# Layer 0's modulation vectors: from TensorE products to VectorE sums inside the window attention

## The chip, the cores and the metric

One core of one Trainium2 chip runs the whole program: a two-layer block of a diffusion transformer, in float32. The metric is device time in microseconds (us) of one execution; the time before is 2756.34 us, the median of three runs. The engines are called by the profile's names: PE (TensorE, matrix products), PEld (its weight loads), DVE (VectorE), ACT (ScalarE), POOL (GpSimd) and SP (SyncE, which here issues every transfer, in order, on one queue).

## The reference, cut to what matters

Both layers scale and shift their normalised activations with a modulation computed from a conditioning vector. There are two streams, the latent tokens (1024) with the vector `c` and the context tokens (256) with `c_ctx`:

```python
mod_l = (jax.nn.silu(c) @ ada_w[layer] + ada_b[layer]).reshape(batch, 1, N_MOD, D_MODEL)
mod_c = (jax.nn.silu(c_ctx) @ ada_w[layer] + ada_b[layer]).reshape(1, 1, N_MOD, D_MODEL)
h_l = modulate(x, norm1_g[layer], mod_l, 0)          # chunks 0 and 1
y_c, y_l = ab_mixer(h_c, h_l, ...)                   # mLSTM and banded window attention
x = x + mod_l[:, :, 2] * y_l                         # chunk 2
x = x + mod_l[:, :, 5] * sq_relu_mlp(modulate(x, norm2_g[layer], mod_l, 3), ...)   # chunks 3, 4, 5
```

`ada_w[layer]` is 1024 x 6144: six chunks of 1024 columns, 24 MB in float32. Chunks 0 and 1 of layer 0 are needed at the very start. The subject here is chunks 2 to 5 of layer 0 (16 MB): chunk 2 at the residual after the mixer, 3 and 4 at the second norm, 5 only when the MLP's second matrix is added to the residual. Layer 1's six chunks are needed after layer 0's MLP.

The window attention of layer 0 has 8 heads of 64 (two per pass, four passes), 10 query blocks of 128 tokens, each block against the context (256 keys) and up to three neighbouring key blocks.

## The kernel before, in words

Tokens lie on the free axis, channels on the 128 partitions. The large products use a split of each float32 operand into a rounded part and a remainder and three products (`mm3`, L436; lines L442 to L444), each 128x128 weights against 512 or 256 columns. SBUF holds one big tile `F` (8592 columns, written in pages of `PG` = 1024 and half pages `H` = 512), tiles `W` for split weights, and `x`, `hhi`, `hlo` for activations. PSUM is one tile of 8 banks; `Banks` hands out banks by letter, and `Area` hands out places of `F` by tag in rotation, so a tile waits for the last reader of the place that it takes.

The stages on the path: `front` (an order written out by hand, with the modulation chunks 0 and 1, keys, values and the first queries), then `swa` (L1808), the window attention with what fills it, then the mLSTM with the output projection, then `mlp` for layer 0 (`mlp_hidden`, then `mlp_out`), then layer 1. Outside the blocks under a manual schedule, the framework's scheduler orders each engine's instructions by its own estimates of their durations; a constraint can be given with `issue_after(ins)`, which puts an instruction behind another one on the same engine and makes no semaphore wait.

In `swa` every one of the 40 (pass, block) turns does this: `scores` (L1816): PE makes up to 8 products into one set of three PSUM banks (L1827 to L1831), DVE takes them out with the band mask and the running maximum (L1835, L1840), ACT makes exponentials (L1850), DVE normalises (L1856). One turn later `values` transposes the result on PE (L1870), ACT and DVE split it (L416, L417 into `ptl`), PE multiplies with the values (L1876, L1877), and DVE adds the two halves (L1881). The score banks are one set, so the next block's products wait until DVE has read the last ones.

Between these turns stand fillers: `queries` (the next pass's projection), `gather` (L1791, the four mLSTM heads' projections, stored to DRAM through a small `ev` tile) and `ada_steps` (L187), which computes the modulation. `rest` (L1891) interleaves `gather` and `ada_steps`; a counter (`total`) spreads all of it evenly over the 40 turns. `ada_steps` takes a 1024-column chunk in four steps. A step loads two 128x1024 pieces of `ada_w` (512 KB each, tag `adaraw`, two places in `F`), makes four products with the two streams' conditioning vectors as 32-column weights (L200), two rows of 128 inputs by two halves of 512 columns side by side in the array, and DVE adds the result up from PSUM (L207; the first step by ACT). At the chunk's end four small products turn the row sums into columns (L212) and DVE adds the bias (L218).

Layer 1's modulation is computed otherwise, by `ada_sums` (L221), in layer 0's `mlp_hidden`: a step loads 128x512 pieces (256 KB, tag `raw`), and DVE multiplies each with one entry of the conditioning vector per partition and adds it to a running sum in PSUM (L233, L235, one instruction per stream and piece, the last one into SBUF, L240); then PE sums over the partitions with a matrix of ones (L249) and DVE adds the bias (L252). Its generator is asked for a step at three places in each pair of hidden blocks (`fill` in `pair`), from the third pair on; DVE also adds up the MLP's own products there (L665, L640).

Of the kernel before, what the change touches and what calls it, by code (L numbers as in the profile page):

```python
# [10 lines left out]
F32 = mybir.dt.float32  # L11
# [8 lines left out]
P = 128  # L20
# [95 lines left out]
class Kernel:  # L116
# [70 lines left out]
    def ada_steps(self, layer, block, wp, tp, psp, tag):  # L187


        nc, a = self.nc, self.a  # L190
        acc = tp.tile([P, 512], F32, tag="adaacc")
        for kk in range(ND // 2):
            ps = psp.tile(tag, "adaps")
            for e in range(2):
                k = 2 * kk + e
                w = wp.tile([P, 1024], F32, tag="adaraw")
                nc.sync.dma_start(w, a["ada_w"][layer, k * P : (k + 1) * P, block * 1024 : (block + 1) * 1024])
                for u in range(2):
                    q = 2 * e + u
                    nc.tensor.matmul(  # L200
                        ps[32 * q : 32 * q + 32, :], self.cs[:, k, :], w[:, u * 512 : u * 512 + 512],
                        start=True, stop=True, tile_position=(0, 32 * q),
                    )
            if kk == 0:
                nc.scalar.activation(acc, ps, AF.Copy)
            else:
                nc.vector.tensor_tensor(acc, ps, acc, op=ALU.add)  # L207
            if kk < ND // 2 - 1:
                yield
        pt = psp.tile(tag, "adapt")  # L210
        for i in range(4):
            nc.tensor.matmul(pt[:, 4 * i : 4 * i + 4], acc[:, i * P : (i + 1) * P], self.asel, start=True, stop=True)  # L212
        c0 = block * 8
        bias = self.v(V_AB + layer * 48 + c0, 8).rearrange("p (u i) -> p i u", i=4)
        src = pt[:, :16].rearrange("p (i u v) -> p i u v", i=4, u=2)
        dst = self.mod[layer][:, c0 : c0 + 8, :].rearrange("p (u i) v -> p i u v", i=4)
        for vv in range(2):
            nc.vector.tensor_tensor(dst[:, :, :, vv], src[:, :, :, vv], bias, op=ALU.add)  # L218
        yield

    def ada_sums(self, layer, block, streams, tp, psp, tag):  # L221


        nc, a = self.nc, self.a
        sums = [psp.tile(t, "adacc") for t in "XY"[:streams]]
        acc = [[tp.tile([P, n], F32, tag=f"acc{v}") for _ in range(512 // n)] for v, n in enumerate((512, 256)[:streams])]
        for k in range(ND):
            w = tp.tile([P, 512], F32, tag="raw")
            nc.sync.dma_start(w, a["ada_w"][layer, k * P : (k + 1) * P, block * 512 : block * 512 + 512])
            for v in range(streams):  # L230
                c = self.cs[:, k, v : v + 1]
                if k == 0:
                    nc.vector.tensor_scalar(sums[v], w, c, None, op0=ALU.mult)  # L233
                elif k < ND - 1:
                    nc.vector.scalar_tensor_tensor(sums[v], w, c, sums[v], op0=ALU.mult, op1=ALU.add)  # L235
                else:
                    n = 512 // len(acc[v])
                    for i, t in enumerate(acc[v]):
                        x = slice(i * n, i * n + n)
                        nc.vector.scalar_tensor_tensor(t, w[:, x], c, sums[v][:, x], op0=ALU.mult, op1=ALU.add)  # L240
            if k % 4 == 3:
                yield
# [1565 lines left out]
    def swa(self, sp, small, tb, psp, wp, mixd, heads, st, qs, band, gates):  # L1808
# [953 lines left out]
```

## Time and profile before

| what | value |
|---|---|
| three runs | 2754.09, 2756.34, 2759.79 us; median 2756.34 |
| profiled execution, its time and its span | 2762.11 us and 2760.3 us |
| mean granted TensorE clock | 0.994 |
| window attention, 150 to 530 us | PE busy 371.4, DVE 229.7, ACT 200.7, POOL 67.1 us of 380 |
| layer 0's hidden MLP, 860 to 1200 us | PE busy 336.2, DVE 211.7, POOL 206.1 us of 340 |
| products of `ada_steps` (L200) | 128 instructions, 164 to 520 us |
| sums of `ada_sums` (L233 to L249) | about 820 to 1170 us |

A float32 product appears as two matrix instructions. Busy time is the union of an engine's instructions. A busy PE isn't a PE at its peak: its instructions are pipelined, so what one costs is read from the distance of starts and not from its length. In the rows of groups the number after the bar is busy time, then the mean of one in ns, then the idle time of the engine just before them and what ended it. In a timeline, `[2.13 <-DVE small L1835]` is idle time before the row and its releaser.

### The profile page before, as it was taken

To read this page: it belongs to the slowest core of one execution; us is meant where nothing else is said; L and a number is where in the kernel's file an instruction comes from. 1 tells how busy PE (TensorE), PEld (TensorE's weight loads), DVE (VectorE), ACT (ScalarE), POOL (GpSimd) and SP (SyncE) were. 2 spreads that over 40 slices of the span, in tenths; PEclk is the share of its full clock that TensorE was granted. 3 is DMA by queue.
4 is the path that set the end of the run, shared out by engine and by line. 5 is a ranking of instruction groups with operands and counts; after the bars stand their busy time and mean duration, and the time that the engine had idled before them with its cause. 6 is when DMAs were issued, how large, how long until landed. Compare 5 with 4: busy or idle time off the path is not lost.

```text
span 2760.3 us, 40910 instructions
## 1 busy us (share of the span) xinstructions
PE 2692.7 (98%) x14757; PEld 2274.0 (82%) x14757; DVE 1882.4 (68%) x3268; ACT 1472.8 (53%) x2604; POOL 1078.8 (39%) x734
## 2 busy tenths in 40 slices
PE   8999999999999999999999999999999999999999
PEld 4787878787888888878888889999988888878877
DVE  5455556578776666558669557888874676666675
ACT  5665454444674444344437557888865554444342
POOL 2422020001246667510002347787774598720000
PEclk9999999999999999999999999999999999999999
DMA  7222223443325676497747610000155255477674
GB/s 246 87 79 91 101 87 124 160 155 109 111 91 193 198 246 217 154 333 272 257 141 259 217 47 20 24 26 20 32 182 167 69 180 194 172 281 264 215 232 148
DMA packets 194756, 427.96 MB, mean 155 GB/s; under 512 B 21176, under 2 KB 47576, under 8 KB 194552
## 3 DMA queue, kind: packets, MB, share of 16 engines
q1 hardware_dynamic: 194552, 425.34, 46.1%
q8 instruction: 116, 1.90, 0.3%
q14 instruction: 88, 0.72, 0.1%
HBM read 322.51 MB, written 102.74 MB: 154 GB/s over the span
## 4 chain that ended last, share of the span: by engine, by line
PE 74%; DVE 6%; DMA 5%; issue 2%; ACT 2%; POOL 1%; SPq 0%; DVEq 0%; POOLq 0%; ACTq 0%
PE psum L610 23%; PE psum L1089 16%; PE psum L442 4%; PE psum L443 4%; PE psum L444 4%; PE psum L2392 4%; PE psum L2582 3%; PE psum L1187 3%; PE psum L2299 3%; DMA hhiraw<-in_w 3%; DVE W L417 1%; PE psum L1870 1%; POOL W L417 1%; PE psum L2457 1%; DVE x L1094 1%
## 5 line engine op out<-in xcount | busy, mean ns | idle before, releaser
L417 POOL TENSOR_TENSOR W<-F,W 128x512 fp32r<-128x512 f32 (+2 forms) x310 | 469.3, 1528 | 514.6 <-ACT W L416 385.9
L1089 PE MATMUL psum<-W,W 128*128 128x512 f32 x2688 | 615.8, 390 | 10.6 <-DVE W L417 4.8
L1089 PEld LDWEIGHTS psum<-W,W 128*128 128x128 f32 x2688 | 502.7, 188 | 123.3 <-DVE W L417 10.7
L610 PE MATMUL psum<-hhi,W 128*128 128x512 f32 (+1 forms) x1600 | 441.9, 356 | 2.5 <-DVE x L665 1.6
L416 ACT ACTIVATE W<-F 128x512 fp32r<-128x512 f32 (+2 forms) x375 | 269.9, 735 | 285.0 <-POOL F L583 98.3
L610 PEld LDWEIGHTS psum<-hhi,W 128*128 128x128 f32 x1600 | 285.0, 189 | 46.3 <-DVE x L665 2.0
L610 PE MATMUL psum<-hlo,W 128*128 128x512 f32 (+1 forms) x800 | 284.3, 355 | 0.0
L416 ACT ACTIVATE W<-hhiraw 128x1024 fp32r<-128x1024 f32 x98 | 103.9, 1061 | 313.1 <-PE psum L1089 189.7
L442 PE MATMUL psum<-hhi,W 128*128 128x512 f32 (+1 forms) x600 | 224.4, 374 | 0.0
L444 PE MATMUL psum<-hhi,W 128*128 128x512 f32 (+1 forms) x600 | 218.3, 364 | 0.0
L443 PE MATMUL psum<-hlo,W 128*128 128x512 f32 (+1 forms) x600 | 218.0, 363 | 0.0
L417 DVE TENSOR_TENSOR W<-hhiraw,W 128x1024 fp32r<-128x1024 f32 x98 | 119.6, 1221 | 73.8 <-ACT W L416 73.2
L583 POOL TENSOR_TENSOR F<-F 128x512 f32<-128x512 f32 x112 | 164.9, 1472 | 12.4 <-DMA F<-in_w 5.4
L610 PEld LDWEIGHTS psum<-hlo,W 128*128 128x128 f32 x800 | 151.2, 189 | 21.4 <-issue 0.2
L1008 DVE TENSOR_TENSOR hhiraw<-hhiraw 128x512 f32<-128x512 f32 x154 | 104.2, 688 | 91.0 <-DMA hhiraw<-in_w 90.1
L409 POOL TENSOR_TENSOR hlo<-F,hhi 128x256 fp32r<-128x256 f32 (+1 forms) x12 | 13.1, 1088 | 301.8 <-ACT F L400 301.8
L442 PEld LDWEIGHTS psum<-hhi,W 128*128 128x128 f32 x600 | 113.7, 190 | 20.3 <-ACT x L416 2.5
L443 PEld LDWEIGHTS psum<-hlo,W 128*128 128x128 f32 x600 | 113.8, 190 | 16.7 <-issue 2.2
L444 PEld LDWEIGHTS psum<-hhi,W 128*128 128x128 f32 x600 | 113.6, 189 | 16.2 <-issue 0.2
L417 DVE TENSOR_TENSOR W<-hloraw,W 128x1024 fp32r<-128x1024 f32 x98 | 122.8, 1253 | 4.0 <-DMA hhiraw<-in_w 4.0
L610 PE MATMUL psum<-x,W 128*128 128x512 f32 x504 | 125.1, 393 | 0.0
L610 PEld LDWEIGHTS psum<-x,W 128*128 128x128 f32 x504 | 95.6, 190 | 20.4
(496 smaller groups left out, 6268.2 us busy)
## 6 DMA issues: line engine op xcount, KB each, us to landing
F<-in_w SPq DMA_DIRECT2D x104, 512.0 KB
hloraw<-hd SPq DMA_DIRECT2D x90, 512.0 KB
hhiraw<-in_w SPq DMA_DIRECT2D x72, 512.0 KB
hd<-F SPq DMA_DIRECT2D x142, 256.0 KB
hhiraw<-in_w SPq DMA_DIRECT2D x116, 256.0 KB
F<-in_ada_w SPq DMA_DIRECT2D x96, 256.0 KB
hd<-x SPq DMA_DIRECT2D x90, 256.0 KB
F<-in_win SPq DMA_DIRECT2D x32, 512.0 KB
```

The source lines that it names most:

```text
L416: nc.scalar.activation(hi, src, AF.Copy)
L417: eng.tensor_tensor(lo, src, hi.bitcast(F32), op=ALU.subtract)
L442: nc.tensor.matmul(ps, sh, mh, start=i == 0, stop=False)
L443: nc.tensor.matmul(ps, sh, ml, start=False, stop=False)
L444: nc.tensor.matmul(ps, sl, mh, start=False, stop=i == n - 1)
L583: add = lambda o, p, q, how: nc.gpsimd.tensor_tensor(o, p, q, op=how)
L610: nc.tensor.matmul(ps, w[i][:, p], B[j][k], start=first and j == 0 and m == 0, stop=last and j == 3 and m == 2)
L1008: tt = lambda o, p, q, how: eng.tensor_tensor(o, p, q, op=how)
L1089: nc.tensor.matmul(bank(base + i), A[u][:, p], B[v], start=first and m == 0, stop=last and m == 2)
L1187: nc.tensor.matmul(bank(k), B[u][:, i * P : i * P + P], A[v][:, half], start=f == 0 and m == 0, stop=f == NFF - 1 and m == 2,)
L2299: nc.tensor.matmul(ps, s[:, c], m[:, j, t0 : t0 + QT], start=j == 0 and i == 0, stop=j == ND - 1 and i == 2)
L2392: nc.tensor.matmul(u.o[:, :QT], v[x], p[y], start=c == 0 and m == 0, stop=c == 2 * NB - 1 and m == 2)
```

## The change

`ada_steps` is deleted. Layer 0's chunks 2 to 5 are now eight half chunks of 512 columns computed by `ada_sums` with both streams: six (512-column blocks 4 to 9) as fillers in the window attention, two (blocks 10 and 11, which are chunk 5) ahead of layer 1's twelve in the hidden MLP. In the attention the running sums lie in SBUF (`F`), not in PSUM; three places of 256 KB take the loads; each DVE sum is put behind the newest score block's normalisation on DVE (`pace`), and the first half chunk's loads behind the front's last store on SP (`behind`). A block in the attention has four steps of two pieces (`marks` 1, 3, 5, 7), asked for after three of five `gather` steps instead of two of five; `total` grows from 66 to 75. In the MLP a block with two streams has three steps of 3, 3 and 2 pieces where it had two of 4 and one for the turn; the turn now rides with the next block's first step.

```diff
-    def ada_steps(self, layer, block, wp, tp, psp, tag):
...
-                w = wp.tile([P, 1024], F32, tag="adaraw")
-                nc.sync.dma_start(w, a["ada_w"][layer, k * P : (k + 1) * P, block * 1024 : (block + 1) * 1024])
-                for u in range(2):
-                    q = 2 * e + u
-                    nc.tensor.matmul(
-                        ps[32 * q : 32 * q + 32, :], self.cs[:, k, :], w[:, u * 512 : u * 512 + 512],
-                        start=True, stop=True, tile_position=(0, 32 * q),
-                    )
...
-    def ada_sums(self, layer, block, streams, tp, psp, tag):
+    def ada_sums(self, layer, block, streams, tp, psp, tag, sums=None, marks=(3, 7), behind=None, pace=nullcontext):
...
+        if sums:
+            acc = [[t] for t in sums]
+        else:
+            sums = [psp.tile(t, "adacc") for t in "XY"[:streams]]
...
         for k in range(ND):
             w = tp.tile([P, 512], F32, tag="raw")
-            nc.sync.dma_start(w, a["ada_w"][layer, k * P : (k + 1) * P, block * 512 : block * 512 + 512])
+            with self.tc.issue_after(behind.ins) if behind else nullcontext():
+                nc.sync.dma_start(w, a["ada_w"][layer, k * P : (k + 1) * P, block * 512 : block * 512 + 512])
+            with pace():
+                for v in range(streams):
+                    c = self.cs[:, k, v : v + 1]
+                    if k == 0:
+                        nc.vector.tensor_scalar(sums[v], w, c, None, op0=ALU.mult)
+                    elif k < ND - 1:
+                        nc.vector.scalar_tensor_tensor(sums[v], w, c, sums[v], op0=ALU.mult, op1=ALU.add)
...
-            if k % 4 == 3:
+            if k in marks:
                 yield
...
+    def ada_pieces(self, pieces, *args, behind=None, **kw):
+
+        for layer, block, streams, marks in pieces:
+            yield from self.ada_sums(layer, block, streams, *args, marks=marks, behind=behind, **kw)
+            behind = None
         yield
...
-            nc.sync.dma_start(ud[0][1][:, s], e)
+            self.fronted = nc.sync.dma_start(ud[0][1][:, s], e)
...
-                nc.vector.tensor_scalar(sc[:, h, :nk], sc[:, h, :nk], nm[:, 5, h : h + 1], None, op0=ALU.mult)
+                paced[0] = nc.vector.tensor_scalar(sc[:, h, :nk], sc[:, h, :nk], nm[:, 5, h : h + 1], None, op0=ALU.mult)
...
-            ada = (s for b in range(2, 6) for s in self.ada_steps(0, b, wp, tb, psp, "A"))
+            F = self.F
+            sums = [tb.tile([P, 512], F32, tag="adaacc"), F[:, 4 * PG + H : 5 * PG]]
+            ad = Area()
+            ad.place("raw", cuts(F, H, 3 * PG, 3 * PG + H, 4 * PG))
+            ada = self.ada_pieces(
+                [(0, b, 2, (1, 3, 5, 7)) for b in range(4, 10)], ad, psp, "A",
+                sums=sums, behind=self.fronted, pace=lambda: self.tc.issue_after(paced[0].ins),
+            )
...
-                if i % 5 in (1, 3):
+                if i % 5 in (0, 2, 3):
...
-        total, done, left = 3 * 3 + 48 - 7 + 16, 0, 0
+        total, done, left = 3 * 3 + 48 - 7 + 25, 0, 0
...
-            steps.append(s for b in range(12) for s in k.ada_sums(1, b, 2 if b < 4 else 1, tp, psp, tag))
+            pieces = [(0, b, 2, (2, 5, 7)) for b in (10, 11)]
+            pieces += [(1, b, 2, (2, 5, 7)) if b < 4 else (1, b, 1, (3, 7)) for b in range(12)]
+            steps.append(k.ada_pieces(pieces, tp, psp, tag))
```

Three places show what this moves. The first is PE in the window attention. Before, a step's four products stand between a block's transposes (`psum<-ident,x`) and the next block's score products (`psum<-KH`, `psum<-KL`):

```order
L1830 MATMUL psum<-KH_579,x_1985 128x384
L1831 MATMUL psum<-KL_581,x_1985 128x384
L1870 MATMUL psum<-ident,x_1096 128x128 x8
L200 MATMUL psum<-F,cs 32x512 x4
L1827 MATMUL psum<-KH_579,x_1984 128x256
L1828 MATMUL psum<-KL_581,x_1984 128x256
L1830 MATMUL psum<-KH_579,x_1984 128x256
```

With the change no such row is left. Six times there are eight short products with the matrix of ones, one half chunk's turn (`psum<-hhi,W` and `psum<-hlo,W` are projections, L1803 to L1807 the score products under their new line numbers):

```order
L419 MATMUL psum<-hhi,W_106 128x256
L420 MATMUL psum<-hlo,W_106 128x256
L421 MATMUL psum<-hhi,W_106 128x256
L220 MATMUL psum<-ones,F 128x2 x8
L1803 MATMUL psum<-KH_579,x_1996 128x256
L1804 MATMUL psum<-KL_581,x_1996 128x256
L1806 MATMUL psum<-KH_579,x_1996 128x384
```

So sixteen groups of four wide products, and four groups of four turns, became six groups of eight turns on PE here.

The second is DVE in the same stage. Before, between the split of the transposed scores (`ptl`), a block's normalisation (L1856) and the next block's scores (L1835), one addition of `ada_steps` (L207):

```order
L1846 TENSOR_TENSOR small<-vec,small 128x2
L207 TENSOR_TENSOR F<-psum,F 128x512
L1853 TENSOR_TENSOR small<-small 128x2
L1854 RECIPROCAL small<-small 128x2
L1881 TENSOR_TENSOR x_1097<-psum,small 64x128
L1856 TENSOR_SCALAR x_1095<-x_1095,small 128x640 x2
L1881 TENSOR_TENSOR x_1097<-psum,small 64x128
L1835 ISA x_1096,small<-psum,kzero,vec 128x256
```

Now (L1832 is the normalisation, L1811 the next block's scores):

```order
L1829 TENSOR_TENSOR small<-small 128x2
L1830 RECIPROCAL small<-small 128x2
L394 TENSOR_TENSOR ptl<-psum,x_1098 128x256
L1832 TENSOR_SCALAR x_1096<-x_1096,small 128x640 x2
L206 SCALAR_TENSOR_TENSOR F<-F,cs 128x512
L1857 TENSOR_TENSOR x_1097<-psum,small 64x128 x2
L206 SCALAR_TENSOR_TENSOR F<-F,cs 128x512 x3
L1811 ISA x_1095,small<-psum,kzero,vec 128x256
```

Four sums stand between a normalisation and the next block's scores; there are 24 such groups in the 40 turns.

The third is SP's queue at the end of the front. Before, two loads of 512 KB stood among the front's weights:

```order
L1599 DMA F<-in_rope 128x1024
L197 DMA F<-in_ada_w 128x1024
L1516 DMA F<-in_win 128x1024
L197 DMA F<-in_ada_w 128x1024
L1516 DMA F<-in_win 128x1024
```

Now the first three, of 256 KB, stand behind the front's last stores and ahead of the band mask (`in_band`):

```order
L1726 DMA u_137<-F 128x512 x2
L1345 DMA F<-in_tri 128x2x128
L199 DMA F<-in_ada_w 128x512 x3
L1348 DMA F<-in_band 128x384
L1781 DMA u_137<-F 128x256
```

The 48 loads of the attention then go two at a time between the stores of `gather` and the weights.

More of the change, by code (lines that the diff above doesn't have):

```diff
@@ L185, in v @@
         return self.vec[:, i : i + n]
-    def ada_steps(self, layer, block, wp, tp, psp, tag):
+    def ada_sums(self, layer, block, streams, tp, psp, tag, sums=None, marks=(3, 7), behind=None, pace=nullcontext):
         nc, a = self.nc, self.a
[L191 to L195, printed above, removed]
-                w = wp.tile([P, 1024], F32, tag="adaraw")
-                nc.sync.dma_start(w, a["ada_w"][layer, k * P : (k + 1) * P, block * 1024 : (block + 1) * 1024])
-                for u in range(2):
-                    q = 2 * e + u
-                    nc.tensor.matmul(
-                        ps[32 * q : 32 * q + 32, :], self.cs[:, k, :], w[:, u * 512 : u * 512 + 512],
-                        start=True, stop=True, tile_position=(0, 32 * q),
-                    )
[L204 to L219, printed above, removed]
@@ L221, in ada_sums @@
-    def ada_sums(self, layer, block, streams, tp, psp, tag):
-        nc, a = self.nc, self.a
-        sums = [psp.tile(t, "adacc") for t in "XY"[:streams]]
-        acc = [[tp.tile([P, n], F32, tag=f"acc{v}") for _ in range(512 // n)] for v, n in enumerate((512, 256)[:streams])]
+        if sums:
+            acc = [[t] for t in sums]
+        else:
+            sums = [psp.tile(t, "adacc") for t in "XY"[:streams]]
+            acc = [[tp.tile([P, n], F32, tag=f"acc{v}") for _ in range(512 // n)] for v, n in enumerate((512, 256)[:streams])]
@@ L227, in ada_sums @@
         for k in range(ND):
             w = tp.tile([P, 512], F32, tag="raw")
-            nc.sync.dma_start(w, a["ada_w"][layer, k * P : (k + 1) * P, block * 512 : block * 512 + 512])
[L230 to L240, printed above, removed]
@@ L241, in ada_sums @@
-            if k % 4 == 3:
+            with self.tc.issue_after(behind.ins) if behind else nullcontext():
[7 more added lines that the diff above has]
+                        nc.vector.scalar_tensor_tensor(sums[v], w, c, sums[v], op0=ALU.mult, op1=ALU.add)
+                    else:
+                        n = 512 // len(acc[v])
+                        for i, t in enumerate(acc[v]):
+                            x = slice(i * n, i * n + n)
+                            nc.vector.scalar_tensor_tensor(t, w[:, x], c, sums[v][:, x], op0=ALU.mult, op1=ALU.add)
@@ L1373, in mixer0 @@
                 wp.place("raw", cuts(self.F, PG, 2 * PG))
-                wp.place("adaraw", cuts(self.F, PG, 3 * PG, 4 * PG))
                 tb.place("ev", cuts(self.F, H, 5 * PG))
```

1 line of the change is left out of this document (added).

## The prediction

> **What bounds the kernel now.** I read the page's busy shares first, then the chain that ended last, then the busy times by stage.
>
> ```profile
> span 2760.3 us, 40910 instructions
> PE 2692.7 (98%) x14757; PEld 2274.0 (82%) x14757; DVE 1882.4 (68%) x3268; ACT 1472.8 (53%) x2604; POOL 1078.8 (39%) x734
> PE 74%; DVE 6%; DMA 5%; issue 2%; ACT 2%; POOL 1%; SPq 0%; DVEq 0%; POOLq 0%; ACTq 0%
> ```
>
> PE is busy in 98% of the span and makes 74% of the chain. That is an average, so the stages that the change touches are read by themselves (columns: PE, PEld, DVE, ACT, POOL busy, granted clock, DMA share, GB/s):
>
> ```profile
> 0.00:150.00 150.00, 137.50 (x727) 92.92 (x728) 77.66 (x167) 88.06 (x162) 52.61 (x40) 0.98 0.47 158
> 150.00:530.00 380.00, 371.35 (x2235) 307.50 (x2234) 229.72 (x770) 200.74 (x455) 67.08 (x43) 0.99 0.30 100
> 860.00:1200.00 340.00, 336.18 (x1823) 291.44 (x1822) 211.74 (x302) 146.43 (x269) 206.07 (x149) 1.00 0.61 204
> ```
>
> In the window attention (150 to 530 us) PE leaves 8.6 us idle of 380, and DVE 150.3. PE is the bound there, with DVE in a loop with it. What DVE waits for is in its groups:
>
> ```profile
> L1835 DVE CUSTOM_DVE_ANT_0 x<-psum,kzero,vec 128x256 f32<-128x256 f32 x76 | 34.2, 481 | 68.2 <-PE psum L1828 68.2
> L207 DVE TENSOR_TENSOR F<-psum,F 128x512 f32<-128x512 f32 x12 | 8.2, 687 | 11.8 <-PE psum L200 11.8
> L1853 DVE TENSOR_TENSOR small<-small 128x2 f32<-128x2 f32 x38 | 7.1, 186 | 32.3 <-ACT x L1850 28.7 <-ACT small L1847 3.6
> ```
>
> Of its 150.3 us, 68.2 are waits for PE's score products and 11.8 for the modulation's products; the other 70.3 are waits inside the softmax (32.3 on the exponentials) and small ones. So DVE has some 80 us to give in this stage and no more; the rest is its own latency.
>
> **What is removed from PE.** Starts of one step's products and of one turn:
>
> ```profile
> 331.19 1.06 PE L200 MATMUL psum<-F,cs 128*32 128x512 f32 x8
> 332.18 0.39 PE L1827 MATMUL psum<-KH,x 128*128 128x256 f32 x1
> ...
> 333.20 1.01 PE L212 MATMUL psum<-asel,F 128*128 128x4 f32 x8
> 334.07 0.64 PE L1870 MATMUL psum<-ident,x 128*128 128x128 f32 x4
> ```
>
> A group of four products (eight instructions) holds PE 332.18 - 331.19 = 0.99 us, since the four run side by side. Three of the sixteen groups are cut in two by another row, and then each piece takes as long as a whole one:
>
> ```profile
> 287.69 1.05 PE L200 MATMUL psum<-F,cs 128*32 128x512 f32 x2
> 288.67 0.38 PE L1877 MATMUL psum<-ptl,VV 128*128 128x256 f32 x1
> 288.98 1.06 PE L200 MATMUL psum<-F,cs 128*32 128x512 f32 x6
> 289.97 0.39 PE L1827 MATMUL psum<-KH,x 128*128 128x256 f32 x1
> ```
>
> So 19 pieces by 0.99 = 18.8 us; bounds 15.8 (16 groups) and 20.2, the busy time of all of L200 in its group's row. Four turns by 0.87 are 3.5. Removed: 22.3 us.
>
> **What is added to PE.** One half chunk with two streams in layer 0's MLP today:
>
> ```profile
> 880.36 0.95 PE L249 MATMUL psum<-ones,F 128*128 128x2 f32 x8
> 881.17 1.03 PE L249 MATMUL psum<-ones,x 128*128 128x2 f32 x8
> 882.06 0.36 PE L610 MATMUL psum<-hhi,W 128*128 128x256 f32 x1
> ```
>
> 882.06 - 880.36 = 1.70 us. Six of them in the attention are 10.2, two in the MLP 3.4. PE's account alone: -22.3 + 10.2 + 3.4 = **-8.7 us**, with the bounds of L200 between -5.7 and -10.1. The PE-bound length of the attention stage goes from 380 to 380 - 22.3 + 10.2 = 367.9 us.
>
> **What is added to DVE in the attention.** Six half chunks by 8 pieces by 2 streams = 96 operations of 128x512 that read two SBUF operands and write SBUF. The kernel before has no such sum in SBUF; the nearest rows are in the front:
>
> ```profile
> L1553 DVE SCALAR_TENSOR_TENSOR F<-F 128x512 f32<-128x512 f32 x8 | 5.5, 689 | 4.1 <-ACT F L1548 4.1
> L1570 DVE SCALAR_TENSOR_TENSOR F<-x,gs,F 128x512 f32<-128x512 f32 x10 | 9.4, 943 | 2.7 <-ACT F L1564 1.9 <-POOL hlo L1539 0.6
> ```
>
> They are the bounds: 0.69 us undisturbed, 0.94 where POOL works beside it. POOL is busy in 35% of the front (52.6 of 150) and in 18% of the attention (67.1 of 380), so I take 0.69 + 0.25 x 18/35 = 0.82. DVE's account of the stage is busy 229.7, less 8.2 (L207), plus 1 for the bias, plus 70.3 of waits that stay, plus 96 sums: 292.8 + 96 x 0.82 = 371.5 us. At 0.69 it is 359.0, at 0.94 383.0. Against PE's 367.9 the two nearly meet; they cross at 0.78 us for a sum. That is the uncertain part of this change. The gap in which the sums were put is this one (a block's normalisation, the two additions, the next scores):
>
> ```profile
> 278.83 1.01 DVE L1856 TENSOR_SCALAR x<-x,small 128x640 f32<-128x640 f32 x2
> 279.97 0.58 DVE L1881 TENSOR_TENSOR x<-psum,small 64x128 f32<-64x128 f32 x2
> 282.31 0.48 DVE L1835 CUSTOM_DVE_ANT_0 x<-psum,kzero,vec 128x256 f32<-128x256 f32 x1 [1.76 <-PE psum L1828]
> ```
>
> 1.76 us are free; a group of four sums takes 2.8 to 3.8, so the next block's scores are taken out 1.0 to 2.0 us late, and behind them wait the split `ptl` and with it PE's value products. In the changed order PE has more projection products ahead of those in many turns, which covers it; some 16 of the 40 turns get no sums and catch up. I take 3.6 us for the account (371.5 - 367.9) and 1.4 for turns where the cover fails: **+5**, bounds 0 (sums at 0.69, all covered) and +15 (383.0 - 367.9).
>
> The Trainium skill ("SBUF — State Buffer", section "Who interferes with whom") says that a DVE operation with two SBUF inputs and a GpSimd operation that reads SBUF can't run together: the second waits for the whole of the first. By that rule each new sum, unlike L207 with one operand in PSUM, can be held back by a POOL split of weights, and it can hold one back; it speaks against the change, and its sum would be nearer the upper bound, -8.7 + 15. The row at 0.94 agrees with it in kind.
>
> **A stall that may go.** In the attention before there is one long stall:
>
> ```profile
> 433.12 1.06 PE L200 MATMUL psum<-F,cs 128*32 128x512 f32 x8
> 436.32 0.38 PE L1827 MATMUL psum<-KH,x 128*128 128x256 f32 x1 [2.13 <-DVE small L1835]
> ...
> 433.02 2.43 DVE L1312 TENSOR_TENSOR x<-x 128x128 f32<-128x128 f32 x1
> ...
> 436.00:448.00 12.00, 11.18 (x44) 9.64 (x45) 6.01 (x27) 2.76 (x11) 0.00 (x0) 0.72 0.50 186
> ```
>
> One DVE operation of the gates took 2.43 us, PE had only L200 to do and stood still for 2.13 us, and then the granted clock was 0.72 over 12 us, which costs 12 x 0.28 = 3.4: together 5.5. In the new order projections stand around that place. The gates' operations stay, so I count half: **-3**, bounds -5.5 and 0. The Trainium skill ("TensorE: Matmul & The Clock Gate", Part 1) gives such a fall to half rate after about 3.4 us of idleness; here 2.13 us and some shorter pauses were enough. What matters is that any new stall of some 2 us on PE costs about 5.5 us.
>
> **The MLP.** Two more half chunks with two streams are 2 x 8 x 2 = 32 operations, by 0.752 us of the first row here 24 us, on a DVE that is idle for 128 of 340 us, 22.0 of it because pieces of `ada_w` came late:
>
> ```profile
> L235 DVE SCALAR_TENSOR_TENSOR psum<-F,cs,psum 128x512 f32<-128x512 f32 x72 | 53.4, 752 | 22.0 <-DMA F<-in_ada_w 21.2
> 856.66 0.96 PE L610 MATMUL psum<-W,W 128*128 128x512 f32 x3 [2.35 <-DVE F L665]
> 850.00:860.00 10.00, 7.65 (x41) 6.49 (x40) 9.86 (x12) 2.90 (x5) 8.59 (x7) 0.88 0.77 268
> 860.00:870.00 10.00, 10.00 (x55) 8.70 (x54) 5.89 (x9) 6.47 (x13) 7.01 (x6) 0.95 0.48 156
> ```
>
> Where two-stream blocks already run, PE loses only this one stall: 2.35 us and 10 x 0.12 + 10 x 0.05 = 1.7 of clock, 4.0 in all. The new steps of 3, 3 and 2 pieces fit three places of loads, where four pieces had to wait for a place; the first steps stay crowded all the same. I take **-1**, bounds +3 and -4. If the cover failed, DVE's 24 us would not appear whole but as stalls of this kind.
>
> **At nothing:** the 4 MB that move from the attention (DMA share 0.30) to the MLP (0.61) take 4 / 204 GB/s = 20 us of 340 and are covered by DMA's idle share. The two loads taken out of the front are behind PE's work there. Loads on SP now wait for DVE's sums where they waited for L200; a store of `gather` or a weight load behind them is late by as much. That is a rival below.
>
> **Sum.** -8.7 + 5 - 3 - 1 = -7.7 us on the profiled execution: 2762.1 goes to 2754.4 (span 2752.6). The median of the runs shown, 2756.34, lies 5.8 us below the profiled one, and the same difference gives **2748.6, forecast 2749 us** (-0.3%). Its own range, from the middle halves of the bounds: 2743 to 2754.
>
> **Rivals.**
>
> 1. *DVE becomes the bound of the attention, slower.* Every sum waits for POOL's splits or holds them up, price 0.94: +15 on PE's account, and two of the late groups stop PE for 2 us with the clock's fall, 2 x 5.5 = 11, no stall recovered: -8.7 + 15 + 11 = +17 at the worst, half of it at 0.88 us; I put it at +9, **2765**. It decides from 0.85 us for a sum on. For it: the two accounts differ by 3.6 us already. Against: POOL's share is half the front's, and 68.2 us of DVE's waits were behind PE.
> 2. *Nothing measurable: SP's queue.* SP stood at loads of `ada_w` nine times before, up to 8.4 us (waits of SP's queue, 100 to 560 us):
>
> ```profile
> SPq L197 <- PE psum L200: 31.0, 9, 8.4
> SPq L433 <- POOL W L417: 51.4, 16, 8.9
> ```
>
> If a load now waits for a sum tied behind a late score block, the weights (L433) behind it come late and PE stops once or twice, 5.5 each: the gain is eaten, **2757**. Against: loads have three places and are used a step later, some 14 us.
> 3. *All of it: the sums hide.* Price 0.69, both stalls gone: -8.7 - 5.5 - 4 = -18, **2738**. For it: DVE at 359.0 against 367.9. Against: DVE would then be busy or bound 98% of the stage.
>
> **Chances.** Forecast 0.42, rival 1 0.21, rival 2 0.20, rival 3 0.17. A measurement of this kernel tells about 0.2% (5.5 us) from no change: faster is below 2750.8, slower above 2761.9. Faster: two thirds of the forecast's case, all of rival 3, a little of rival 2: 0.49. Slower: most of rival 1: 0.20. The same: 0.31. The range for 8 in 10 cuts off the far parts of rivals 1 and 3: 2737 to 2764.
>
> **What would show it.** PE's own waits in the attention that DVE ended were these, before:
>
> ```profile
> PE psum L1827 <- DVE small L1835: 2.1, 1, 2.1
> PE psum L1876 <- DVE ptl L417: 1.8, 2, 1.3
> PE psum L1877 <- DVE ptl L417: 1.7, 1, 1.7
> ```
>
> PE between 150 and 530 us: no products at 0.99 us, twelve half turns of 0.85. The new sums' row: a mean near 0.8 us or below supports the sum, over 0.85 rival 1, together with next to no idle time of DVE before the scores (68.2 before) and PE waits on `ptl` well above the 1.8 and 1.7 here. The granted clock by 10 us: a second fall beside the one at 436 is rival 1 or 2, and the releaser (DVE or a weight) says which. In the MLP, DVE's idle time on `in_ada_w` should fall, and PE's starts at two more turns cost 1.7 each. The prediction is wrong if the attention gets longer than 380 us, or if the gain comes from a stage that this text doesn't name.

## The result and the profile after

The changed kernel takes **2774.84 us** (median of 6 runs, 2773.87 to 2779.32); the kernel before, run beside it, 2755.73. The ratio is 1.0069, with a 95% interval of 1.0057 to 1.0081: 19 us slower, where 2749 was forecast and 2737 to 2764 was the range. The profiled execution took 2779.3 us.

The page of the changed kernel: span, busy shares, engines of the chain that ended last.

```profile
span 2777.3 us, 41044 instructions
PE 2693.4 (97%) x14725; PEld 2286.2 (82%) x14725; DVE 1976.2 (71%) x3394; ACT 1470.5 (53%) x2600; POOL 1081.9 (39%) x734
PE 75%; DVE 10%; DMA 6%; issue 4%; ACT 3%; POOL 1%; SPq 0%; DVEq 0%; POOLq 0%; ACTq 0%
```

PE's busy time is what it was (2692.7 before), the span is 17 us longer: the loss is idle time and slow clock, not work. DVE's share of the chain went from 6 to 10%.

To see where, I took the start of each PE instruction in both traces (the k-th of its line in the one, the k-th in the other) and the difference of the two. It grows from +3.1 us at 140 us to +5.7 at the start of the MLP (780 us of the kernel before), +11.2 at 1140, +23.8 at 1190 and +20.1 at 1300 us; then it stays to 2500. The attention, which should have become 12 us shorter, gave nothing, and the MLP lost 14 us. (The +3.1 is in the first 60 us; the profiles of the kernels below show 0.4 to 3.3 there, the second run, whose front has no edit, 2.2. I don't count it to the change.)

The changed kernel by stage (PE, PEld, DVE, ACT, POOL busy, granted clock, DMA share, GB/s):

```profile
150.00:530.00 380.00, 360.95 (x2141) 310.12 (x2140) 285.78 (x827) 197.19 (x444) 68.44 (x43) 0.98 0.26 85
860.00:1200.00 340.00, 326.41 (x1760) 284.22 (x1761) 229.72 (x331) 137.62 (x259) 205.42 (x149) 0.97 0.62 204
```

**The attention.** PE's work fell by 371.35 - 360.95 = 10.4 us, and its idle time rose from 8.6 to 19.0, by the same 10.4. DVE rose from 229.7 to 285.8. The new lines among DVE's groups (150 to 540 us) and what they stand beside (lines are 24 lower than before: L1811 was L1835, L1821 was L1845):

```profile
L206 DVE SCALAR_TENSOR_TENSOR F<-F,cs 128x512 f32<-128x512 f32 x72 | 60.2, 881 | 0.6
L1811 DVE CUSTOM_DVE_ANT_0 x<-psum,kzero,vec 128x256 f32<-128x256 f32 x76 | 33.8, 479 | 29.4 <-PE psum L1804 29.3
L1821 DVE TENSOR_SCALAR small<-small 128x2 f32<-128x2 f32 x38 | 12.9, 340 | 0.1
L211 DVE SCALAR_TENSOR_TENSOR F<-F,cs 128x512 f32<-128x512 f32 x12 | 8.4, 744 | 0.0
```

A sum (L206) takes 0.881 us in the mean, over the 0.85 that the prediction set as the mark of its rival 1. But it isn't a price of 0.88: the median is 0.747, and six of the 84 sums take 1.8 to 2.9 us. One of them, with what ran beside it and what waited for it:

```profile
319.10 2.93 DVE L206 SCALAR_TENSOR_TENSOR F<-F,cs 128x512 f32<-128x512 f32 x1
319.11 2.38 POOL L394 TENSOR_TENSOR W<-F,W 128x1024 fp32r<-128x1024 f32 x1 [27.18 <-PE psum L1807]
...
321.96 0.57 DVE L1857 TENSOR_TENSOR x<-psum,small 64x128 f32<-64x128 f32 x2
...
322.67 0.81 PE L1846 MATMUL psum<-ident,x 128*128 128x128 f32 x4 [1.98 <-DVE x L1857]
323.13 0.78 PE L421 MATMUL psum<-hhi,W 128*128 128x512 f32 x1
```

The window around it (columns as in the windows above):

```profile
318.00:328.00 10.00, 8.03 (x36) 6.44 (x35) 9.81 (x21) 3.38 (x7) 2.38 (x1) 0.83 0.41 119
```

The sum began with POOL's split of a weight, and ended 0.54 us after the split's end (319.11 + 2.38 = 321.49; 319.10 + 2.93 = 322.03): it stood still for the whole of it. Behind it on DVE were the two additions L1857, behind those PE's transposes; PE stood for 1.98 us, and the clock of these 10 us was 0.83, 1.7 us more. The same happens to the small operations of the softmax: L1821 has a mean of 340 ns for a median of 160. Counting every DVE instruction between 150 and 530 us that runs beside one of POOL and takes over 0.3 us more than the median of its group: before 8, held for 9.3 us in all; changed 18, 25.2 us.

PE's waits between 150 and 560 us:

```profile
PE psum L1853 <- DVE ptl L394: 4.0, 4, 1.6
PE psum L1852 <- ACT x L393: 3.7, 5, 2.1
PE psum L1846 <- DVE x L1857: 2.9, 2, 2.0
PE psum L1852 <- DVE ptl L394: 2.7, 3, 1.2
PE psum L1846 <- DVE x L1832: 2.4, 2, 1.5
...
PE psum L2566 <- DVE W L394: 0.5, 1, 0.5
...
PE psum L2566 <- ACT W L393: 0.4, 1, 0.4
```

All large ones are DVE's (or ACT's copies, which wait in the same loop). For weights (`W`) PE waited 0.9 us in all, so in the attention the rival on SP's queue is out.

**The MLP.** One wait makes the loss. PE's waits from 860 to 1200 us:

```profile
PE psum L220 <- DVE F L211: 9.1, 1, 9.1
PE psum L587 <- DVE F L642: 2.5, 1, 2.5
```

And the window around it, before and changed:

```profile
1150.00:1190.00 40.00, 39.02 (x211) 33.58 (x210) 23.56 (x34) 14.33 (x26) 12.80 (x9) 1.00 0.60 193
1150.00:1190.00 40.00, 30.94 (x153) 26.45 (x153) 16.60 (x25) 10.80 (x21) 14.67 (x12) 0.83 0.32 106
```

PE stood for 9.1 us at the turn of the very last half chunk, and the clock of these 40 us is 0.83: 40 x 0.17 = 6.8 us more. Before, PE was busy for 39.0 of the same 40 us, at a clock of 1.00. The chain of work that ended last, inside that stretch (start, duration, what):

```profile
1154.17 0.32 SPq L618
...
1155.04 0.45 SPq L199
1155.48 0.04 issue
1155.53 5.41 DMA F<-in_ada_w
...
1161.82 0.76 DVE psum L206
1162.58 0.60 DVE F L642
1163.18 0.02 issue
1163.20 0.64 ACT F L599
...
1164.78 0.07 SPq L602
...
1164.95 2.90 DMA F<-in_ada_w
```

Read downwards: stores of row sums (L618) held SP; the first four pieces of `ada_w` came behind them; DVE's sums waited for the pieces; behind the sums stood an MLP operation (L642), behind it ACT, behind ACT a store (L602), and behind that store on SP the last four pieces. The two steps of this chunk fall into two neighbouring calls of the filler, with L642 between them.

### The profile page after: what moved, and what is told of

The parts are those of the page before. It is cut to its first block, busy times and chain, and to the rows that moved or that the text cites. A ratio compares the mean times of both kernels' runs of the same rounds, so it can differ in the third digit from the quotient of the medians.

```text
span 2777.3 us, 41044 instructions
## 1 busy us (share of the span) xinstructions
PE 2693.4 (97%) x14725; PEld 2286.2 (82%) x14725; DVE 1976.2 (71%) x3394; ACT 1470.5 (53%) x2600; POOL 1081.9 (39%) x734
## 4 chain that ended last, share of the span: by engine, by line
PE 75%; DVE 10%; DMA 6%; issue 4%; ACT 3%; POOL 1%; SPq 0%; DVEq 0%; POOLq 0%; ACTq 0%
PE psum L587 21%; PE psum L1066 14%; PE psum L421 5%; PE psum L419 5%; PE psum L420 5%; PE psum L2376 4%; DMA hhiraw<-in_w 4%; PE psum L1164 3%; PE psum L2566 3%; PE psum L2283 3%; DVE W L394 2%; DMA F<-in_ada_w 1%; PE psum L1846 1%; PE psum L220 1%; PE psum L1438 1%
## 5 line engine op out<-in xcount | busy, mean ns | idle before, releaser
L587 PEld LDWEIGHTS psum<-hlo,W 128*128 128x128 f32 x800 | 152.5, 191 | 21.5 <-issue 0.2
L206 DVE SCALAR_TENSOR_TENSOR psum<-F,cs,psum 128x512 f32<-128x512 f32 x120 | 87.7, 750 | 38.0 <-DMA F<-in_ada_w 37.3
```

The costliest lines, as they stand in the source:

```text
L587: nc.tensor.matmul(ps, w[i][:, p], B[j][k], start=first and j == 0 and m == 0, stop=last and j == 3 and m == 2)
```

## The experiments

Two theories. **A**: the MLP's loss is this one stall, made by late loads. **P**: the attention's loss is made by POOL's splits of weights, which hold up DVE's operations on SBUF, sums and softmax alike, at places where PE waits for DVE. The main rival: DVE is simply too full, and the held operations only show it. In the readings, a signed number with a place, such as -4.6 at the start of the MLP, is the difference of PE's starts to the profiled kernel before, as above. Code is shown shortened: `...` stands for what isn't printed, and what only follows from an edit, such as the count `total`, isn't printed either. Each kernel's time is the median beside the median of the kernel before in the same batch.

**1. The steps of the last chunks shifted by one call.**

```diff
-... else (1, b, 1, (3, 7)) for b in range(12)]
+... else (1, b, 1, (2, 5, 7) if b == 10 else (3, 7)) for b in range(12)]
```

> The changed kernel with one number tuple altered: the last but one half chunk of layer 1 (block 10) is summed in three steps (2, 5, 7) where it had two (3, 7). Nothing is removed or added; every later step falls one call later, so that the last chunk's eight sums no longer fall into two neighbouring calls. Theory A (the two traces put 13.5 of the 17 us into one stall of PE at the last turn in layer 0's MLP, 9.1 us of waiting and 13.7 us at half clock): the stall goes, 2759 to 2764. Theory B (the MLP's stall is an accident of the profiled execution, the lasting loss is the attention's sums held up by POOL): no change, 2771 to 2778.

2768.43 us beside 2755.01 (1.0047, 1.0029 to 1.0065). Half of what A said, and in neither's range. The wait of PE at the last turn is 4.5 us instead of 9.1; the MLP loses 7.0 us (from +4.8 to +11.8), not 14.4. So the place matters, but it isn't all.

**2. The MLP part alone.** Attention by products (blocks 2 to 4), MLP as in the change.

```diff
-ada = self.ada_pieces(...)
+ada = (s for b in range(2, 5) for s in self.ada_steps(0, b, wp, tb, psp, "A"))
```

> The change's MLP part alone: the attention computes blocks 2 to 4 by products as before (block 5 is gone from it), the MLP is the changed one with its 14 half chunks. By products 4 groups of 0.99 us and one turn of 0.87 less in the attention, -5. Theory A: the MLP's +14 is all here, 2755.7 - 5 + 14 = 2765 (2760 to 2769). Theory B (the loss is in the attention): 2755.7 - 5 + 3 = 2754 (2750 to 2757).

2763.06 beside 2755.01 (1.0029, 1.0020 to 1.0039), as A said. -4.6 at the start of the MLP, +8.3 behind it: 12.9 lost in it, with the same stall (8.5 us). The MLP part does its damage whatever the attention does.

**3. The attention part alone**, with block 5 by products ahead of the sums and the MLP's steps as before.

```diff
+ada = chain(self.ada_steps(0, 5, wp, tb, psp, "A"), ada)
-total, done, left = 3 * 3 + 48 - 7 + 25, 0, 0
+total, done, left = 3 * 3 + 48 - 7 + 29, 0, 0
```

> The change's attention part alone: blocks 2 to 4 are summed by DVE in the attention as in the change, block 5 is computed there by products ahead of them, and the MLP has the 12 half chunks and steps of before. Theory A: the attention gives about +1 on the profile where -12 of PE work was taken out, and block 5's five pieces come on top, 2755.7 + 1 + 5 = 2762 at most, 2754 to 2763. Theory B: nearly all the loss is here, 2768 to 2775. The forecast's own terms would give 2755.7 - 7.3 + 5 - 3 = 2750.

2774.19 beside 2755.01 (1.0064, 1.0045 to 1.0082): a miss of A, and not a clean answer for B. The attention loses 16.7 us (from +3.3 at 140 to +20.0 at 780 us), and its long stop stands at the end: four steps had no turn left and ran there one after another.

```profile
544.64 2.73 DVE L240 SCALAR_TENSOR_TENSOR F<-F,cs 128x512 f32<-128x512 f32 x4
547.29 0.48 DVE L1853 CUSTOM_DVE_ANT_0 x<-psum,F,small 128x256 f32<-128x256 f32 x1
547.69 0.08 DVE L1853 DVE_READ_ACCUMULATOR2_ANT small<- 128x1 f32 x1
549.12 1.41 DVE L240 SCALAR_TENSOR_TENSOR F<-F,cs 128x512 f32<-128x512 f32 x2 [1.34 <-DMA F<-in_ada_w]
...
551.59 0.69 PE L1883 MATMUL psum<-ident,x 128*128 128x128 f32 x2 [5.56 <-DVE ptl L430]
```

PE had no products left to fill with there, and the sums ahead of the split `ptl` cost it a stop of 5.56 us. The run shows that, and says little of the change.

**4. POOL's large splits of the attention away**, in `queries` and in `gather` alike.

```diff
-w = self.unit(self.wp0, a["win0"][U_QB + pr])
+w = self.unit(self.wp0, a["win0"][U_QB + pr], eng=self.zero_lo())   # ScalarE copies with scale 0
```

> The changed kernel with the 15 low halves of weights that POOL makes in the attention's stage (128x1024, some 2.5 us each) replaced by a copy with scale zero on ScalarE: these low halves are zero, so the output has lower precision; POOL keeps only the small splits of the gates. Theory P (seven of the 84 sums take 1.7 to 2.9 us because a POOL split runs beside them, and PE's stalls follow them): the sums' mean falls from 0.88 to 0.75 us, PE's idle time between 150 and 530 us from 19 to about 10 us, the clock falls there from four to one or none: 2774.8 - 12 = 2763 (2758 to 2767). Rival (the groups of four sums are late by themselves, undisturbed 4 x 0.75, or the 15 us more on ScalarE take the gain): 2770 to 2780, with the stalls still there.

2754.42 beside 2755.01 (0.9988, 0.9975 to 1.0001). 20 us faster than the change, more than P said (2758 to 2767), with the order of PE and DVE nearly untouched. Sums 0.761 us, no fall of the clock between 150 and 530 us, and the start of the MLP at -13.5. Of the MLP's stall nothing went (8.3 us). The output's lower precision comes from the zero halves; the matmuls are as many.

**5. The same splits in four.**

```diff
-self.nc.gpsimd.tensor_tensor(lo, src, hi, op=op)
+for i in range(4):
+    c = slice(i * 256, i * 256 + 256)
+    self.nc.gpsimd.tensor_tensor(lo[:, c], src[:, c], hi[:, c], op=op)
```

> The changed kernel with each of the 15 POOL splits of 128x1024 weights in the attention's stage cut into four of 128x256; the output is unchanged. Theory P (a sum waits for the whole of the POOL instruction that runs beside it, so what counts is how long one is): no sum over some 1.5 us, mean at most 0.80 us (0.88 in the change), clock falls in the attention two or fewer, 2774.8 - 12 = 2763 (2757 to 2768). Rival Q (what counts is POOL's total time at the memory, which four smaller ones don't shorten): a sum meets several quarters in turn, mean still 0.85 or more, 2771 to 2778.

2768.75 beside 2757.09 (1.0043, 1.0028 to 1.0058). Between P and Q, and by the sums' mean (0.850) nearer Q: 33 DVE operations are held instead of 18, for 21.5 us in all (25.2), only five of them over 1 us. Shorter instructions make shorter stops, not fewer.

**6 and 7. All eight half chunks in the attention, the MLP as before**, without and with POOL's splits in four.

```diff
-[(0, b, 2, (1, 3, 5, 7)) for b in range(4, 10)]
+[(0, b, 2, (1, 3, 5, 7)) for b in range(4, 12)]
-if i % 5 in (0, 2, 3):
+if i % 5 < 4:
```

> The change's MLP part undone and its attention part whole: all eight half chunks of blocks 2 to 5 are summed by DVE in the attention, the MLP has the 12 half chunks and the steps of the kernel before. 32 sums more in the attention than in the change. Theory A+P (MLP +13 by its one stall, attention a loss by POOL splits): the MLP falls back to +0, the attention gets 3.4 us of turns and a third more of held-up sums: 2755.7 + 3 (front) + 1 + 3.4 + 6 = 2769 (2764 to 2775). Rival (the attention's DVE is simply full: 286 + 27 us busy): 2778 or more. The forecast's terms would give 2750.

> Both together: all eight half chunks in the attention, the MLP as before, and the attention's POOL splits cut into four. Theory P: PE's account of -8.7 us comes out in the attention with few held-up sums: 2749 to 2757, which would be no slower than the kernel before. Rival Q or a full DVE: 2765 to 2778.

2768.43 and 2756.84 beside 2757.09 (1.0045, 1.0030 to 1.0060; and 1.0001, 0.9991 to 1.0010). In both the MLP loses nothing (-1.7 and -2.1 from 780 to 1300 us): that part of A holds from this side too. In the first, 23 operations of DVE are held, 30.9 us in all, and its sums are nearly free of it (L206: 0.761): it hits the small operations, one of 160 ns for 4.02 us. With quarters 31 are held, for 16.5 us, and 11.6 us are won.

**8. The MLP's steps one pair earlier.**

```diff
-fill(3)
+fill(2)
...
-fill(2)
+fill(1)
...
-fill(2)
+fill(1)
```

> The changed kernel with all its modulation steps in layer 0's MLP one pair of hidden chunks earlier (the calls begin at pair 2 where they began at pair 3), so that the last half chunk ends a pair before the place of the stall. Theory A (the stall belongs to that pair, where the stores of its row sums hold SP for 8 us ahead of the last chunk's loads): the 13.5 us go, at most 3 come back at the crowded start of the MLP: 2763 (2759 to 2768). Rival (any last chunk whose eight loads come in two neighbouring calls stalls like this, or the start stalls in its place): 2770 to 2778.

2769.28 beside 2757.09 (1.0044, 1.0029 to 1.0059). Between A and its rival, again half: PE's wait at a turn is 1.8 us, but 2.4 and 2.3 us of waits stand elsewhere, and the MLP loses 7.8. That speaks for pieces in two neighbouring calls making trouble where they fall, not in that pair alone, but what made these two waits isn't shown.

**9. The low halves on VectorE**, all eight half chunks in the attention, the MLP as before.

```diff
-w = self.unit(self.wp0, a["win0"][U_QB + pr])
+w = self.unit(self.wp0, a["win0"][U_QB + pr], eng=nc.vector)   # gather's units too
```

> All eight half chunks in the attention and the MLP as before (the run with 2768), with the attention's 15 low halves of weights made by VectorE itself where POOL made them: 15 x 1.22 us more on DVE, and nothing of POOL's large splits beside it; the output is unchanged. Theory P (POOL's splits hold DVE's operations with two SBUF operands, sums and small softmax operations alike, and that makes PE's stalls): operations of 160 ns that took up to 4 us are gone, and 2768 - 14 + 4 = 2758 (2752 to 2764). Rival (DVE is full, the held operations only show it): 313 us busy plus 18 is still more, 2775 or above.

**2746.02** beside 2755.25 (0.9970, 0.9961 to 0.9980): faster than both kernels and than P's range (2752 to 2764), with 18 us more of work on DVE. This is what decides against "DVE is full". Its sums (DVE's groups, 100 to 540 us):

```profile
L206 DVE SCALAR_TENSOR_TENSOR F<-F,cs 128x512 f32<-128x512 f32 x96 | 66.8, 746 | 0.7
```

And its window of the attention:

```profile
150.00:530.00 380.00, 370.49 (x2266) 321.27 (x2265) 318.65 (x923) 204.66 (x469) 32.14 (x30) 0.99 0.33 107
```

DVE is busy for 318.7 of 380 us and PE idles for 9.5, half of the change's 19.0 with DVE at 285.8.

**10. Sums in steps of two** on the seventh run, asked for at twice as many places.

```diff
-[(0, b, 2, (1, 3, 5, 7)) for b in range(4, 12)]
+[(0, b, 2, range(8)) for b in range(4, 12)]
```

> All eight half chunks in the attention, POOL's splits in four, the MLP as before (the run with 2756.8), with the sums in steps of two operations where there were four, spread over twice as many places. If groups of four (3.0 us for a gap of 1.8) make the next scores late, as the forecast's term of 1.4 us had it, fewer waits of PE on DVE: 2750 (2746 to 2754). If the group's size is nothing, since PE has products ahead of the scores: 2755 to 2759.

2757.34 beside 2755.25 (1.0011, 1.0001 to 1.0021). The size of a group makes no difference here.

**11. The change without the tie** (`pace`, which puts each sum behind a score block's normalisation).

```diff
-sums=sums, behind=self.fronted, pace=lambda: self.tc.issue_after(paced[0].ins),
+sums=sums, behind=self.fronted,
```

> The changed kernel without the tie: the sums are no longer held behind the normalisation of a score block, so the scheduler puts them as early as their loads and places allow. Theory P says nothing of the order, only of what runs beside POOL: 2768 to 2781, the held operations' total about as before. If the tie is what keeps the sums from delaying the scores: 2780 or above. If the tie itself is the loss (SP's loads wait for sums that are tied late, 74.5 us of waiting in SP's queue at these loads): 2765 or below.

2762.18 beside 2755.25 (1.0034, 1.0022 to 1.0046), 12 us faster than the change: the number of the third theory, a miss for P's. The gain is in the attention (-4.6 at the start of the MLP, the change +5.7) and, to a lesser part, in the MLP (8.3 us lost instead of 14.4). But the third theory's reason, loads that wait for tied sums, is not seen: in the change DVE's sums L206 idle for 0.6 us in all (their row above), so no piece came late. Here the sums' mean is 0.774 and 17.8 us are held, 25.2 in the change. The scheduler's order of PE and DVE is another one throughout, so this run alone doesn't settle whether the tie sends sums beside POOL's splits or does something else.

**12. The kernel before with quarters.**

> The kernel before with nothing but POOL's 15 splits of the attention cut into four. It parts what quarters do by themselves from what they do for the sums. Theory P: the softmax's small operations were already held there, 5.3 us in all (five of 38 at L1845, up to 2.4 us), of which perhaps half reaches PE: 2754 (2750 to 2757), so that quarters are worth 2 or 3 us here and 12 where the sums stand. Rival (quarters shorten something that has nothing to do with the sums, such as the weights' arrival): 2746 or below, the same 12 us.

2752.02 beside 2755.25 (0.9998, 0.9988 to 1.0008): no change, so what quarters won in the seventh run has to do with the sums.

**13. The last chunk without its loads.** Of layer 1's last half chunk only the first piece is loaded, and all its sums read that one.

```diff
-w = tp.tile([P, 512], F32, tag="raw")
-...
-nc.sync.dma_start(w, ...)
+if k == 0 or (layer, block) != (1, 11):
+    w = tp.tile([P, 512], F32, tag="raw")
+    ...
+    nc.sync.dma_start(w, ...)
```

> The changed kernel with seven of the eight loads of the very last half chunk (layer 1, block 11) left out: its eight sums all read the first piece, so this one chunk's modulation is wrong; every DVE and PE instruction stays. If the stall is made by loads that come late (SP held by stores of row sums, then by one store that waits for DVE, which waits for loads): PE's wait of 9.1 us at the last turn goes to under 1 and the half clock of 10 to 14 us with it, 2774.8 - 13 = 2762 (2758 to 2766). If DVE's 24 us more of sums are the cause: 2771 or more.

2763.83 beside 2756.37 (1.0029, 1.0019 to 1.0040), 11 us faster than the change; the order on the engines is unchanged. PE's waits of 820 to 1210 us:

```profile
PE psum L588 <- DVE F L643: 3.1, 1, 3.1
PE psum L221 <- DVE F L212: 1.7, 1, 1.7
PE psum L588 <- DVE x L643: 1.7, 1, 1.7
```

With the same sums on DVE the wait of 9.1 us is 1.7, and the MLP costs 1.8 us (from +5.7 to +7.5) instead of 14.4. The loads were the cause.

**14 and 15. The low halves on VectorE alone**, in the kernel before and in the change.

> The kernel before with nothing but the 15 low halves of the attention's weights made by VectorE where POOL made them (a control). Theory P: there are no sums to be held up, the small operations held at L1845 (5.3 us) come free, 18 us more on a DVE that idles 150 us: 2752 (2748 to 2757). Rival (VectorE is better for these halves whatever the sums): 2746 or below, as in the run with sums.

> The changed kernel as it is, with nothing but these 15 low halves moved to VectorE; the output is unchanged. Theory P: the attention's loss goes as in the run whose low halves were zero (-20), 18 us more on DVE cost at most 5, and the MLP's stall stays: 2757 (2752 to 2762). Rival (DVE becomes the bound: 288 busy less 10 plus 18): 2770 or more.

2751.28 beside 2756.37 (0.9984, 0.9972 to 0.9995) and 2755.45 beside 2756.37 (0.9997, 0.9986 to 1.0008). The same edit is worth about 5 us in the kernel before and 19 in the change (2774.8 to 2755.5), with the order on PE and DVE nearly untouched. The changed kernel's start of the MLP goes from +5.7 to -14.9, that of the kernel before to -5.7. Sums and low halves among DVE's groups of the fifteenth run (150 to 540 us):

```profile
L206 DVE SCALAR_TENSOR_TENSOR F<-F,cs 128x512 f32<-128x512 f32 x70 | 50.0, 762 | 0.6
...
L394 DVE TENSOR_TENSOR W<-F,W 128x1024 fp32r<-128x1024 f32 x19 | 23.6, 1244 | 3.8 <-ACT W L393 3.8
```

And PE's longest waits (150 to 560 us):

```profile
PE psum L1852 <- ACT x L393: 2.2, 4, 1.0
PE psum L1945 <- ACT hhis L1958: 1.9, 3, 1.1
PE psum L1852 <- DVE ptl L394: 1.5, 2, 1.0
```

11 operations are held for 8.8 us, in place of 18 for 25.2, and no single wait of these is over 1.1 us.

**16. The ninth run without the tie.**

> The run with 2746 (all eight half chunks in the attention, low halves by VectorE, MLP as before) without the tie of the sums behind the score blocks. If the tie costs only because it puts sums beside POOL's splits: no change, 2743 to 2749. If it costs in itself (SP's loads wait for tied sums): 2738 or below. If it protects the scores: 2750 or above.

2750.10 beside 2756.37 (0.9973, 0.9960 to 0.9985). The time lies at the edge of the branch "it protects the scores" (2750 or above), but the kernel before was 1.1 us slower in this batch too, and the two intervals overlap (0.9970 with the tie). So where POOL has no large splits no cost of the tie shows, which supports, without proving it, that in the change it costs by what it puts beside the splits.

## Why the prediction was wrong, point by point

- **PE's account (-8.7)** held as an account of work: PE's busy time in the attention fell by 10.4 us, where -22.3 + 10.2 = -12.1 was put. What it is worth in time shows only where POOL's splits are out of the way, in the fourteenth and fifteenth runs: from 140 to 780 us the changed kernel goes from +1.2 to -14.9 (-16.1), but the kernel before, which keeps its products, goes from +2.7 to -5.7 (-8.4). So 7.7 us of the 12.1 come out, by one profile of each.
- **The price of a sum (0.82)**: wrong in form, more than in size. I put 0.82 between an undisturbed row and a disturbed one, by POOL's share of the stage. There is no such mean price: a sum takes 0.75, or it stands for the rest of a 2.4-us split. The row at 0.94 (L1570 in the front) had this form already: nine of its ten operations take about 0.75 us, and one, begun at 21.62 us beside a split of POOL's, 2.72.
- **"Took +5 (0 to +15)"** is the step that failed. From 140 to 780 us the change went from +3.1 to +5.7, that is +2.6; with -12.1 for PE's work and -5.5 for the stall that went, what the sums took is 2.6 + 12.1 + 5.5 = 20.2 us, over the upper bound. Against the same kernel with the splits on DVE the change lost 18.7 us there (+2.6 and -16.1); 8.4 of these the splits cost the kernel before as well. DVE's account (371.5 us busy and waiting against PE's 367.9) was the wrong measure: the ninth run has 33 us more on DVE and loses nothing like it. What counted is that DVE in this stage is in PE's loop, so that one operation held for 2 us can become a wait of PE of 2 us and a fall of the clock, 1.7 us each, and that the softmax's own small operations are held a little longer too (L1821: 340 ns for 301 before). By the Trainium skill ("SBUF — State Buffer", section "Who interferes with whom") an operation with two SBUF inputs and a GpSimd operation that reads SBUF exclude each other, and the second waits for the whole of the first. The trace agrees with the holding (2.93 us beside a split of 2.38). The prediction told this as a case "nearer the upper bound, -8.7 + 15", and took POOL's share of the stage for its sum.
- **The 1.4 us for groups of four**: there was nothing (tenth run).
- **The stall at 433 us (-3)** went altogether; -5.5 was the right end, but the stall was misread. "The gates' operations stay" took the 2.43 us of L1312 for its own length. It stood beside a split of POOL's and ended 0.14 us after it (433.02 + 2.43 = 435.45 against 432.95 + 2.36 = 435.31), in the kernel before:

```profile
432.95 2.36 POOL L417 TENSOR_TENSOR W<-F,W 128x1024 fp32r<-128x1024 f32 x1 [12.82 <-ACT W L416]
433.02 2.43 DVE L1312 TENSOR_TENSOR x<-x 128x128 f32<-128x128 f32 x1
```

  In the fourteenth run, with the splits on DVE, the same operation takes 0.29 us, and the fall of the clock behind it is gone. So the trace of before showed what was to come: a split holds an operation of DVE, PE stops for 2 us, the clock falls. In the changed kernel four falls stand elsewhere in the attention, at 268, 296, 323 and 361 us.
- **The MLP (-1, bounds +3 and -4)** is the second step that failed. The stage lost 14.4 us, of which 3.4 were the two turns in PE's account; this term measured 11.0. "The new steps of 3, 3 and 2 pieces fit three places of loads" looked at the places only. The other chunks, with one stream, had lost their third step, and no queue was followed past them: SP's loads stand behind stores, one of these waits for DVE, and DVE waits for loads. Without the last chunk's loads the MLP costs 1.8 us, less the 3.4 of the turns -1.6: inside the bounds. The two steps make the miss: 12.7 us in the attention (-10.1 put, +2.6 measured) and 12.0 in the MLP (+2.4 and +14.4), together the 24.7 between the -7.7 forecast and the +17.0 of the profiled spans.
- **At nothing, the moved 4 MB**: DMA's share is 0.62 (0.61 before), so bytes were not the trouble; the place of their issue was.
- **Rival 1** (2765, POOL holds the sums, decides from 0.85 us) had the holding, the mark and, for the attention alone, the time: without the MLP's late loads the change takes 2763.8. Its heading, DVE as the bound, was not so: the ninth run has more on DVE and is faster. It had a chance of 0.21. **Rival 2** had its queue in the wrong stage: SP did make a loss, in the MLP. **Rival 3** (2738, the sums hide) came in no run of the change itself; the ninth run, 2746, is the nearest.
- **What would show it**: the attention got longer by 2.6 us (PE's starts from +3.1 at 140 to +5.7 at 780 us); the mean over 0.85, the waits on `ptl` above 1.8 and 1.7 (4.0 and 2.7) and the second fall of the clock did, and DVE's idle time on `in_ada_w` in the MLP rose where it should have fallen (27.7 us at L206, 21.2 at L235 before). One sign of rival 1 did not come: DVE still idled 29.4 us before the scores (68.2 before), which is not next to none.

What stays open: how much of the tie's 12 us is chance, since the order it makes is another one; and whether moving products to sums is worth anything beside moving the splits, since 0.9970 and 0.9984 (ninth and fourteenth runs) have intervals that overlap.

## What to carry to other kernels

Before work is moved to VectorE, list what GpSimd runs in the same stage: an operation on SBUF costs not its mean but, now and then, the rest of a GpSimd instruction, and on a path that TensorE waits for that is paid again as clock. Try the shared work on VectorE itself; it was 18 us more of work and 19 us less of time here. When a step of a side job is dropped or merged, follow its loads through the issuing queue to the last one: a load behind a store that waits for the engine that waits for the load makes a stall that no account of busy time shows.

## What the runs showed of the hardware

- A DVE operation of 128x2 with one SBUF input, some 0.16 us, took 4.02 us beside a GpSimd split and two memsets that followed one another (sixth run, in order of start):

```profile
389.01 2.39 POOL L396 TENSOR_TENSOR W<-F,W 128x1024 fp32r<-128x1024 f32 x1 [9.56 <-ACT W L395]
389.60 4.02 DVE L1823 TENSOR_SCALAR small<-small 128x2 f32<-128x2 f32 x1
391.32 1.18 POOL L1229 MEMSET mr<- 128x1280 f32 x1
...
392.42 1.18 POOL L1229 MEMSET ir<- 128x1280 f32 x1
```

  It ends (393.62) 0.02 us after the second memset: small size, one input and a GpSimd that only writes were no protection. Theory P spoke of operations with two SBUF operands only.
- The holding goes both ways, but it hurts one side: in the sixth run a split at 464.5 us took 2.97 us beside a sum of 0.75, yet the splits' mean in the attention is 2.44 us before and 2.48 in the change, with 84 sums in the stage. GpSimd's instructions are the long ones, and in this stage PE waited for none of them.
- Four GpSimd instructions in place of one held nearly twice as many DVE operations (33 for 18) for nearly the same sum of time (21.5 for 25.2 us).
- Around a stop of TensorE of 1.98 us the mean clock of 10 us was 0.83, around one of 9.1 us that of 40 us was 0.83: the longer stop came with a loss of 6.8 us of clock, four times the shorter one's 1.7.
